# Building the shifted convolution input inside SBUF, with a reordered output projection and column-tiled modulation, in an eight-core encoder block

## The chip, the cores and the metric

The kernel runs on the 8 cores of one Trainium2 chip; every core executes the same program on its own data. The metric is the device time of one execution, in microseconds (us), on the slowest core. Most executions agree within 0.3%, but some fall into a slower state in which the cores of one die (cores 0 to 3 or 4 to 7) are granted a lower TensorE clock. Only fast runs are compared here; where a median quoted below holds a slow run, the text says so.

## The reference, cut to what matters

Each core handles 16384 positions in 32 tiles of 512, in five sequences of 16, 4, 4, 4 and 4 tiles. All widths below are channels.

```python
mod = silu(c) @ w_ada + b_ada;  shift, scale, gate = split(mod, 3)
h = rmsnorm(x, norm_g) * (1 + scale) + shift            # 1024
p = h @ w_in                                            # 3584
a_in, a_b, a_c, a_z, b_v, b_g, b_z = split(p)           # 512 each
y_a = a_b * dwconv3(a_c * a_in) * silu(a_z)
u   = dwconv31(b_v * sigmoid(b_g)) + conv_b_b           # 31 taps, zero padded
y_b = silu(head_layernorm(u)) * silu(b_z)
out = rmsnorm(x + gate * (concat(y_a, y_b) @ w_out), final_g)
```

Two things matter. The 31-tap convolution of tile i needs 15 positions of the neighbouring tiles, so it can only run once the GLU (`u = b_v * sigmoid(b_g)`) of tile i+1 is complete. And the output row needs its own mean square before it can be stored.

## The kernel before

The traces show the engines run their instructions in program order (VectorE's below are an example). A helper records each operation and adds the semaphore waits, so the order of the Python statements is the order on each engine. TensorE does the input projection (w_in), the convolution, the layer-norm sums and the output projection (w_out).

The convolution multiplies 32 channels x 4 shifted copies (128 rows of contraction) by a 128x32 weight block, 8 times with different offsets. The array V with its four shifted copies is made through a scratch array in DRAM:

```python
def u_store(i):                       # 1 DMA: u of this tile to DRAM
    T.dma("sync", ... out=U_d[:, c:c + NT] ..., in_=u[:], reads=[("u", i % 2)], writes=[("U", i)])

def v_load(i):                        # 4 DMAs: V from DRAM, row group k shifted by k
    for k in range(4):
        T.dma("sync", ... out=V[32*k:32*k+32, :, :],
              in_=U_d[:, c + k:c + k + NT + 28].rearrange("(g c) t -> c g t", c=32))
```

Zero padding between the sequences is written to that scratch once, at the start, by six stores, all of which write the same tracked key, so that each waits for the one before:

```python
for s in range(nseq + 1):
    T.dma("sync", ... out=U_d[:, c0:c0 + PAD]..., in_=zpad[:], writes=["Upad"], semkey="upad")
```

The output projection makes eight half blocks (4 blocks of 128 positions x 2 halves of 512 columns). The transposes of the next tile's normalised input stand between the first four. A block's finish (mean square, power, scale, store) is recorded one block late:

```python
def stage_d(i, nxt):
    fin = []
    for sub in range(4):
        for h in range(2):
            if nxt is not None and sub < 2:
                a_T_group(nxt, (sub*2 + h)*2); a_T_group(nxt, (sub*2 + h)*2 + 1)   # transposes
            bank = PB.next()                                          # one of 6 PSUM banks
            for kc in range(8): matmul(bank, yT[:, kc, ...], w_out_sb[:, kc, ...])
            vector: tmp = bank * gate;  gpsimd: xbuf += tmp
        fin.append(block)
        if len(fin) > 1: d_finish(fin.pop(0))     # the finish of the block before
    while fin: d_finish(fin.pop(0))

def d_finish(...):
    scalar: ssE = sum(xbuf**2);  vector: msE = ssE/D + eps
    gpsimd: rsE = msE ** -0.5;   vector: xbuf = xbuf * rsE * fg;  sync: store
```

The main loop, cut, with `prev = i - 1` and `nxt = i + 1`:

```python
a_load(nxt)                                # x of the next tile
for j in range(4): glu(i, j)               # 64 matmuls, u of tile i
u_store(i); v_load(prev); d_loads(prev)
for j in range(4):
    a1(i, j)                               # 64 matmuls, group A inputs
    if j == 0: a_compute(nxt)              # normalisation: ScalarE squares, GpSimd scaling
# conv_b(0..3) of prev, mixed with matmuls of tile i ("a2", "zb") and layer norm
stage_d(prev, nxt)
```

## Time and profile before

| | before |
|---|---|
| time, median of 3 runs (lowest to highest) | 3340.89 us (3325.13 to 3380.62, the last a slow one, 1.7% above the lowest) |
| profiled run, slowest core | 3350.3 us |
| TensorE busy | 2547.4 us, 76% |
| TensorE waiting for V | 582.7 us |
| first convolution matmul starts | 222.57 us |
| average period of one tile after that | 99.75 us |

The first lines are from the page: busy time by engine (part 1), then two groups of matmuls (part 5) with their busy time, mean ns of one, and the idle time before them with what ended most of it.

```profile
PE 2547.4 (76%) x14704; PEld 1122.2 (33%) x14704; DVE 1096.5 (33%) x1718; ACT 1325.9 (40%) x2180; POOL 740.7 (22%) x773
...
L454 PE MATMUL pb<-hT,w_in_sb 128*128 128x512 bf16 x7168 | 1604.3, 382 | 39.6 <-ACT tp L487 37.5
L541 PE MATMUL pb<-V,WC 128*32 128x512 bf16 x4096 | 296.6, 441 | 582.7 <-DMA V<-u_scratch 582.7
```

TensorE (PE) is by far the busiest engine; the others are at 40% or less. What keeps TensorE from being busy is the wait for V. The view of TensorE's waits lists them: who waited, for whom, then us in total, times, longest us.

```profile
PE pb L541 <- DMA V<-u_scratch: 582.7, 32, 26.7
PE pb L607 <- POOL yT L582: 111.4, 64, 4.9
PE pb L454 <- ACT tp L487: 37.5, 1, 37.5
...
PE ptr L308 <- ACT hT L317: 2.6, 3, 1.1
```

The load of V costs about 18 us in each of 32 tiles; the output projection waits 3.5 us a tile for GpSimd's last yT products; and there is one hole of 37.5 us. The timeline of one tile on TensorE shows the first two. Its columns are start, duration, instruction, count, and in brackets the idle time before it with its releaser.

```profile
1526.00 3.61 PE L541 MATMUL pb<-V,WC 128*32 128x512 bf16 x32 [17.65 <-DMA V<-u_scratch]
...
1533.56 1.91 PE L541 MATMUL pb<-V,WC 128*32 128x512 bf16 x32
...
1563.84 0.38 PE L607 MATMUL pb<-w_out_sb,yT 128*128 128x512 bf16 x1 [2.71 <-POOL yT L582]
```

After the wait the first convolution group takes 3.61 us where the second takes 1.91: the granted clock there is 0.50.

VectorE at the end of the same output projection, whose matmuls end at 1580.1:

```profile
1577.49 1.28 DVE L612 TENSOR_TENSOR tp<-pb,gate_bc 128x512 f32<-128x512 f32 x2
...
1581.66 1.28 DVE L635 SCALAR_TENSOR_TENSOR xb<-xb,rsE,fg_bc 128x1024 f32<-128x1024 f32 x1 [2.83 <-POOL rsE L633]
1582.86 1.28 DVE L612 TENSOR_TENSOR tp<-pb,gate_bc 128x512 f32<-128x512 f32 x2
...
1589.18 1.28 DVE L635 SCALAR_TENSOR_TENSOR xb<-xb,rsE,fg_bc 128x1024 f32<-128x1024 f32 x1 [0.80 <-POOL rsE L633]
```

The scaling of one block (L635) waits for GpSimd's power, and the next block's gate multiplies (L612) stand behind it, but they already follow 5.4 us later (1577.49 to 1582.86), and the last block ends at 1590.46, 10.4 us after the matmuls.

Last, the start. The sync engine's DMA issue queue (SPq), then TensorE:

```profile
60.60 48.45 SPq L362 DMA_DIRECT2D u_scratch<-zpad  x6
...
109.77 3.46 SPq L285 DMA_DIRECT2D xb<-x  x4
```

```profile
125.97 23.38 PE L454 MATMUL pb<-hT,w_in_sb 128*128 128x512 bf16 x96 [37.46 <-ACT tp L487]
```

The six zero-pad stores hold the queue for 48 us, tile 1's x is issued only after them, and TensorE stands still for 37.5 us.

### The profile page before, as it was taken

To read this page: it belongs to the slowest core of one execution; us is meant where nothing else is said; L and a number is where in the kernel's file an instruction comes from. 1 tells how busy PE (TensorE), PEld (TensorE's weight loads), DVE (VectorE), ACT (ScalarE), POOL (GpSimd) and SP (SyncE) were. 2 spreads that over 40 slices of the span, in tenths; PEclk is the share of its full clock that TensorE was granted. 3 is DMA by queue.
4 is the path that set the end of the run, shared out by engine and by line. 5 is a ranking of instruction groups with operands and counts; after the bars stand their busy time and mean duration, and the time that the engine had idled before them with its cause. 6 is when DMAs were issued, how large, how long until landed. Compare 5 with 4: busy or idle time off the path is not lost.

```text
span 3350.3 us, 45102 instructions; the slowest of 8 cores (3297.0 to 3350.3 us)
## 1 busy us (share of the span) xinstructions
PE 2547.4 (76%) x14704; PEld 1122.2 (33%) x14704; DVE 1096.5 (33%) x1718; ACT 1325.9 (40%) x2180; POOL 740.7 (22%) x773
## 2 busy tenths in 40 slices
PE   7567787677796788797877788767788677778783
PEld 2223333233343333343333343333334333333331
DVE  1122333233333333333333343323233333333333
ACT  1123444433443433444442444443344343344333
POOL 3002222122222122222212221212222212222212
PEclk9788998888998898898888899888899888899896
DMA  9744323344322443422344423344432344432323
GB/s 191 145 84 108 91 75 76 84 109 109 100 70 60 96 109 109 105 66 66 96 102 115 109 73 94 71 96 109 109 92 81 63 99 109 109 95 77 65 71 102
DMA packets 159060, 317.22 MB, mean 95 GB/s; under 512 B 14570, under 2 KB 105834, under 8 KB 158836
## 3 DMA queue, kind: packets, MB, share of 16 engines
q1 hardware_dynamic: 149332, 304.90, 36.0%
q0 software_dynamic: 9504, 9.44, 2.1%
q8 instruction: 127, 2.08, 0.3%
q14 instruction: 97, 0.79, 0.1%
HBM read 239.73 MB, written 84.00 MB: 97 GB/s over the span
## 4 chain that ended last, share of the span: by engine, by line
PE 49%; DMA 28%; ACT 11%; issue 5%; SPq 3%; POOL 2%; DVE 2%; ACTq 0%; DVEq 0%; POOLq 0%
PE pb L454 26%; DMA V<-u_scratch 19%; PE pb L607 13%; PE pb L541 7%; DMA u_scratch<-u 6%; SPq L478 3%; ACT L571 2%; ACT tp L573 2%; ACT tp L578 2%; PE ptr L308 2%; DMA u_scratch<-zpad 1%; POOL yT L582 1%; ACT tp L574 1%; ACT L575 1%; PE pb L552 1%
## 5 line engine op out<-in xcount | busy, mean ns | idle before, releaser
L454 PE MATMUL pb<-hT,w_in_sb 128*128 128x512 bf16 x7168 | 1604.3, 382 | 39.6 <-ACT tp L487 37.5
L454 PEld LDWEIGHTS pb<-hT,w_in_sb 128*128 128x128 bf16 x7168 | 702.6, 98 | 905.9 <-issue 95.5
L541 PE MATMUL pb<-V,WC 128*32 128x512 bf16 x4096 | 296.6, 441 | 582.7 <-DMA V<-u_scratch 582.7
L607 PE MATMUL pb<-w_out_sb,yT 128*128 128x512 bf16 x2048 | 516.7, 404 | 111.4 <-POOL yT L582 111.4
L582 POOL TENSOR_TENSOR yT<-tp,gb 128x512 bf16<-128x512 f32 x128 | 145.0, 1154 | 1604.0 <-ACT tp L578 1604.0
L546 ACT ACTIVATE sq<-pb,cbb_sb 128x512 bf16<-128x512 f32 x128 | 87.3, 682 | 904.9 <-PE pb L541 904.9
L614 POOL TENSOR_TENSOR xb<-tp,xb 128x512 f32<-128x512 f32 x256 | 323.9, 1265 | 340.4 <-DVE tp L612 304.8
L508 DVE TENSOR_TENSOR ga<-pb,tp 128x512 bf16<-128x512 f32 x128 | 88.5, 692 | 894.1 <-PE pb L454 783.6
L541 PEld LDWEIGHTS pb<-V,WC 128*32 128x32 bf16 x4096 | 113.6, 107 | 747.8 <-issue 685.0
L607 PEld LDWEIGHTS pb<-w_out_sb,yT 128*128 128x128 bf16 x2048 | 206.8, 104 | 368.1 <-issue 182.2
L629 ACT ACTIVATE tp<-xb 128x1024 bf16<-128x1024 f32 x128 | 135.0, 1055 | 366.9 <-POOL xb L614 366.9
L612 DVE TENSOR_TENSOR tp<-pb,gate_bc 128x512 f32<-128x512 f32 x256 | 170.5, 686 | 278.1 <-PE pb L607 243.8
L635 DVE SCALAR_TENSOR_TENSOR xb<-xb,rsE,fg_bc 128x1024 f32<-128x1024 f32 x128 | 164.4, 1284 | 272.7 <-POOL rsE L633 272.7
L529 DVE SCALAR_TENSOR_TENSOR tp<-t,caT_sb,tp 128x512 f32<-128x512 bf16 x256 | 193.0, 754 | 28.4 <-DVE tp L526 0.9
L292 ACT ACTIVATE xs<-xb 128x1024 bf16<-128x1024 f32 x128 | 135.1, 1056 | 92.3 <-DMA xb<-x 87.3
L317 ACT ACTIVATE hT<-ptr,shT,gsT 128x512 bf16<-128x512 bf16 x124 | 96.2, 776 | 164.2 <-PE ptr L308 164.2
L489 DVE TENSOR_TENSOR t<-pb,tp 128x512 bf16<-128x512 f32 x128 | 88.9, 694 | 208.5 <-PE pb L454 157.6
L297 POOL TENSOR_TENSOR rsA<-msA,mhalf 128x4 f32<-128x4 f32 x32 | 32.5, 1017 | 537.7 <-DVE msA L295 537.7
L577 DVE TENSOR_TENSOR tp<-tp 128x512 f32<-128x512 f32 x128 | 85.5, 688 | 199.1 <-ACT tp L574 199.1
L487 ACT ACTIVATE tp<-pb 128x512 f32<-128x512 f32 x128 | 74.0, 591 | 185.1 <-PE pb L454 179.2
L300 POOL TENSOR_SCALAR xs<-xb,rsA 128x1024 bf16<-128x1024 f32 x128 | 140.9, 1119 | 7.4 <-POOL rsA L297 6.7
L463 ACT ACTIVATE tp<-pb 128x512 f32<-128x512 f32 x128 | 72.5, 590 | 135.1 <-PE pb L454 134.8
(70 smaller groups left out, 1609.1 us busy)
## 6 DMA issues: line engine op xcount, KB each, us to landing
xb<-x SPq DMA_DIRECT2D x256, 512.0 KB, 9.0
V<-u_scratch SPq DMA_DIRECT2D x128, 540.0 KB, 15.2
y<-xb SPq DMA_DIRECT2D x128, 512.0 KB, 2.9
u_scratch<-u SPq DMA_DIRECT2D x32, 512.0 KB, 8.2
xb<-w_ada SPq DMA_DIRECT2D x24, 512.0 KB, 5.2
w_in_sb<-w_in POOLq DMA_DIRECT2D x14, 512.0 KB, 25.5
gate_bc<-gate_scratch SPq DMA_DIRECT2D x5, 512.0 KB, 5.1
w_out_sb<-w_out POOLq DMA_DIRECT2D x4, 512.0 KB, 51.0
```

Source lines behind the costliest of these rows:

```text
L292: T.op("scalar", lambda e, xbuf=xbuf, sub=sub: e.activation(out=xs[:, sub, :], in_=xbuf[:], func=AF.Square, accum_out=ssA[:, sub:sub + 1]) ...
L300: T.op("gpsimd", lambda e, xbuf=xbuf, sub=sub: e.tensor_scalar(out=xs[:, sub, :], in0=xbuf[:], scalar1=rsA[:, sub:sub + 1], scalar2=1.0, o ...
L454: T.op("tensor", lambda e, bank=bank, kc=kc: e.matmul(bank[:], lhsT=w_in_sb[:, kc, col0:col0 + 128], rhs=hT[:, kc, :], start=(kc == 0), st ...
L478: T.dma("sync", lambda e, k=k: e.dma_start(out=V[32 * k:32 * k + 32, :, :], in_=U_d[:, c + k:c + k + NT + 28].rearrange("(g c) t -> c g t" ...
L529: T.op("vector", lambda e, k=k: e.scalar_tensor_tensor(out=acc[:], in0=t1[:, j, k:k + NT], scalar=caT[:, j * KA + k:j * KA + k + 1], in1=a ...
L541: T.op("tensor", lambda e, p=p, g=g: e.matmul(bank[32 * g:32 * g + 32, :], lhsT=WC[:, (j * 4 + g) * 8 + p, :], rhs=V[:, j * 4 + g, 4 * p:4 ...
L582: T.op("gpsimd", lambda e, cc=cc, gsrc=gsrc, j=j: e.tensor_tensor(out=yT[:, 4 + j, :], in0=cc[:], in1=gsrc, op=ALU.mult), reads=[ckey, gke ...
L607: T.op("tensor", lambda e, bank=bank, kc=kc, sub=sub, h=h: e.matmul(bank[:], lhsT=yT[:, kc, sub * 128:(sub + 1) * 128], rhs=w_out_sb[:, kc ...
L612: T.op("vector", lambda e, tmp=tmp, bank=bank, h=h: e.tensor_tensor(out=tmp[:], in0=bank[:], in1=gate_bc[:, h * NT:(h + 1) * NT], op=ALU.m ...
L614: T.op("gpsimd", lambda e, tmp=tmp, xbuf=xbuf, h=h: e.tensor_tensor(out=xbuf[:, h * NT:(h + 1) * NT], in0=tmp[:], in1=xbuf[:, h * NT:(h + ...
L629: T.op("scalar", lambda e: e.activation(out=jb[:].bitcast(BF16), in_=xbuf[:], func=AF.Square, accum_out=ssE[:, c:c + 1]), reads=[xkey], wr ...
L635: T.op("vector", lambda e: e.scalar_tensor_tensor(out=xbuf[:], in0=xbuf[:], scalar=rsE[:, c:c + 1], in1=fg_bc[:], op0=ALU.mult, op1=ALU.mult),
```

## The change

Its intent is to take DRAM out of the way from u to V. u gets room for its neighbours' 15 positions (544 columns). Twelve DMAs copy u, shifted, from SBUF to SBUF, in runs of about 4 KB per partition, and four unshifted blocks are copied by VectorE. With this the zero-pad stores go. The output projection first does contraction halves 0 to 3 (y_a, ready early) of the first four half blocks, with transposes between, and then all the rest, so as not to wait for the last yT. The modulation uses four 32-column tiles of the array at once.

The V path:

```diff
-def u_store(i): ... U_d <- u          # 1 DMA
-def v_load(i):  ... V <- U_d          # 4 DMAs, 1 KB rows
+def u_halo(i):                        # 15 columns to and from the neighbour tile
+    T.op("gpsimd", tensor_copy(out=up[:, :, NT+15:NT+30], in_=u[:, :, 15:30]))
+    T.op("gpsimd", tensor_copy(out=u[:, :, 0:15], in_=up[:, :, NT:NT+15]))
+def v_fill(i):
+    for k in range(4):
+        for g in range(4):
+            sh = 2 * ((k - g) % 4)
+            if k == g: T.op("vector", tensor_copy(V[32*g:32*g+32, g], u[32*g:32*g+32]))
+            else:      T.dma("sync", V[32*k:32*k+32, g] flat [0:4*UW-sh] <- u[32*g:32*g+32] flat [sh:4*UW])
```

The output projection:

```diff
-            if nxt is not None and sub < 2: two transposes groups
-            for kc in range(8): matmul
-            evacuate (gate multiply, add)
-        fin.append(block)
-        if len(fin) > 1: d_finish(*fin.pop(0))
+for n in range(4):
+    if nxt is not None:
+        a_T_group(nxt, 2*n); a_T_group(nxt, 2*n + 1)
+    d_mm(n, range(4))
+for n in range(8):
+    d_mm(n, range(4, 8) if n < 4 else range(8))
+    d_evac(n)                # gate multiply, add, and for h == 1 at once: d_finish(...)
```

The last line hides a side effect: the finish of a block is no longer one block late. The main loop and the start:

```diff
-a_load(nxt)
 for j in range(4):
     glu(i, j)
-u_store(i); v_load(prev); d_loads(prev)
+    if j == 1: a_compute(nxt)
+u_halo(i); v_fill(prev); a_load(i + 2); d_loads(prev)
 ...
     a1(i, j)
-    if j == 0: a_compute(nxt)
-zero-pad stores to U_d
+memset of both u buffers
+a_load(1)                # at the start, ahead of the weight loads
-mod_piece: matmul(bank[0:nseq, :], lhsT=scT[:, kc, :] (5 columns), rhs, ...)          # fp32
+matmul(mbank[32*q:32*q+32, :], lhsT=scT[:, kc, :] (32 columns), rhs, tile_position=(0, 32*q))
```

(The weight table of the convolution is reordered to match the new shifts; the bias and the transposes of the modulation follow the new layout.)

## The prediction

> **What bounds it now.** TensorE, with holes. Page part 1: TensorE 2547 of 3350 us, ScalarE 40%, VectorE 33%. Waits view: 582.7 us before the 31-tap convolution, 32 times, released by the load of V from the DRAM scratch; 111.4 us in the output projection, released by GpSimd's last yT products. One tile in the timeline (1526-1620 us; period about 100): convolution section 33, projection 21, GLU and A inputs 29, wait for V 18. In the wait, u goes to DRAM (8-9 us), then V comes back in 1 KB rows, queued with x loads (13-23 us). Afterwards the first convolution group takes 3.61 instead of 1.91 us, the next 16 matmuls 4.0 instead of 3.6: 2 us of cold clock, granted 0.50 (windows view). That agrees with the Trainium skill, "TensorE: Matmul & The Clock Gate", Part 1: an idle array restarts at half rate.
>
> **The V path.** u is complete 15 us after the GLU matmuls start; V is wanted at 29. Twelve copies of 139 KB: 0.45 us each to issue (small loads in the trace), so 5.4, then 3 to land (y stores: 2.9). The skill's "SBUF — State Buffer", Door 1, gives 32 partitions 8 of 16 ports, about 218 GB/s: 3.8 to 7.6 us of transfer in all, an estimate no run shows yet. Together 8-10 us where 31 were. The four VectorE copies: 0.6 us each.
>
> **Where part is lost.** (1) The halo copies stand on GpSimd behind the next tile's normalisation (5.4 us), whose ScalarE squares (5 us) now stand between the second and third tanh. (2) A row block's finish now follows its own evacuation at once. VectorE works in order, so the next block's gate multiply waits for multiply 0.7, two GpSimd adds 2.7, square 1.25, mean 0.15, power 0.55, scale 1.3 plus semaphores: 7.3 us per block instead of 5.4. The four end 19 us after the projection's matmuls instead of 10.5. PSUM banks come free late, TensorE stalls about 7 us inside the GLU, u is complete only near 25. Halo copies end at 30, V lands at 38; the convolution starts 38-40 us after the projection instead of 47.
>
> **Projection order.** Worth almost nothing. Before the second of four transpose pairs TensorE needs a transpose bank that ScalarE empties only after the second norm pair and the z gates (timeline: 1563.96-1564.74), the same moment as the last yT (1564.8). I expect the 111 us to become waits of transposes on ScalarE, 3.5-4 us a tile.
>
> **Start.** Six zero-pad stores hold the DMA issue queue 48 us; tile 1's x waits behind them, then ScalarE, then TensorE (37.5 us). That goes. Column tiling takes 32 fp32 gate matmuls (12 us) nearly out of tile 1; the first modulation is bound by its weight loads: 1-2 us. First convolution at 160 instead of 222 us. The tail gains nothing.
>
> **Sum.** 30 periods save about 8.5 us each (18 wait + 2 cold - 7 bank stalls - 2 to 3 remaining wait - 1.5 new cold clock): 250. Start 60. Tail +4. 3341 - 306 = about 3030 us; 8 in 10 between 2880 and 3140. Faster by over 2%: 0.96; within 2%: 0.03; slower: 0.01.
>
> **What will show it.** Wait for V below 120 us in total; GLU matmuls waiting for evacuations 4-8 us a tile; VectorE waiting for GpSimd's power above 4 us per block; transposes waiting for ScalarE near 110 us; no 37.5 us hole.
>
> **What would make it wrong.** SBUF copies that serialise on few ports (+8 us a tile, 3270); slow VectorE copies; a block chain that overlaps better than I think (near 2800); a clock throttled once TensorE is denser (dense stretches now get 1.00).

## The result, and the profile after

| | before | after |
|---|---|---|
| time, median | 3335.17 us (4 runs, one of them slow at 3380.62) | 3130.31 us (4 runs, 3127.92 to 3134.56) |
| ratio of fast runs | 1 | 0.9397 (95%: 0.9365 to 0.9428) |
| profiled run, slowest core | 3350.3 us | 3129.9 us |
| TensorE busy | 2547.4 us | 2618.9 us |
| first convolution | 222.57 us | 168.72 us |
| average period of one tile | 99.75 us | 94.15 us |

A ratio is the mean time of one kernel's fast runs over that of the other's fast runs in the same rounds, so it is not quite the ratio of the medians quoted. The outputs were correct, as in all runs below. The time lies inside the predicted range, 10 us from its upper end and 100 us above the predicted 3030.

The difference of the profiled spans, 220.4 us, divides so: start 53.9 (222.57 − 168.72), 30 periods of 5.60 each (168), the last interval 4.2, and 5.6 lost after the last tile's convolution starts (55.3 to 60.9).

The page of after, same lines:

```profile
PE 2618.9 (84%) x14724; PEld 1137.7 (36%) x14724; DVE 1209.6 (39%) x1848; ACT 1325.1 (42%) x2178; POOL 784.9 (25%) x838
...
L444 PE MATMUL pb<-hT,w_in_sb 128*128 128x512 bf16 x7168 | 1665.6, 390 | 200.3 <-DVE tp L617 158.3
...
L542 PE MATMUL pb<-V,WC 128*32 128x512 bf16 x4096 | 313.9, 423 | 102.8 <-DMA V<-u 100.9
```

The same 7168 input-projection matmuls are busy for 61 us longer (1665.6 against 1604.3) and the same convolution matmuls for 17. TensorE did no more of this work; most of the extra time is a lower clock. The clock records say how much: at 0.50 TensorE was busy for 340 us (before 272), which costs half of that time, and at 0.81 for 140 us (before none), which costs 3/16 of it. That makes 196 us against 136, so 60 of the 72 us by which TensorE's busy time grew. (The mean granted clock of the span, 0.919 against 0.883, hides this: before stood at 0.50 for 788 us, but 516 of them were waits.) That is why its busy share, 84%, overstates the gain. The Trainium skill, "Trainium Kernel Development and Optimization", Best Practices, says to judge the distance to the peak by MFU (the share of peak arithmetic) and weight-load busy share, not by matmul busy share; PEld rose only from 33% to 36%.

TensorE's waits in after:

```profile
PE pb L444 <- DVE tp L617: 158.3, 58, 3.5
PE ptr L303 <- ACT hT L312: 126.3, 33, 4.5
PE pb L542 <- DMA V<-u: 100.9, 40, 28.8
...
PE pb L607 <- POOL yT L583: 3.7, 4, 1.6
```

The wait for V fell from 582.7 to 100.9 us; without the first (6.6) and last (28.8) it is 65.5 over 30 tiles, 2.2 us a tile. The projection's 111.4 us on yT fell to 3.7, but 126.3 us of transposes waiting for ScalarE stand in their place. And 158.3 us are new: GLU matmuls waiting for a PSUM bank until VectorE's gate multiply (L617) has emptied it. The timeline of TensorE from the end of a projection (224.97) to the convolution:

```profile
224.97 3.62 PE L444 MATMUL pb<-hT,w_in_sb 128*128 128x512 bf16 x16
231.04 3.61 PE L444 MATMUL pb<-hT,w_in_sb 128*128 128x512 bf16 x16 [2.45 <-DVE tp L617]
238.15 22.82 PE L444 MATMUL pb<-hT,w_in_sb 128*128 128x512 bf16 x96 [3.50 <-DVE tp L617]
263.15 4.24 PE L542 MATMUL pb<-V,WC 128*32 128x512 bf16 x32 [2.19 <-DMA V<-u]
```

VectorE in the same stretch:

```profile
230.21 1.28 DVE L617 TENSOR_TENSOR tp<-pb,gate_bc 128x512 f32<-128x512 f32 x2
235.17 0.15 DVE L642 TENSOR_SCALAR msE<-ssE 128x1 f32<-128x1 f32 x1 [3.68 <-ACT tp L640]
236.12 1.28 DVE L646 SCALAR_TENSOR_TENSOR xb<-xb,rsE,fg_bc 128x1024 f32<-128x1024 f32 x1 [0.80 <-POOL rsE L644]
237.32 1.28 DVE L617 TENSOR_TENSOR tp<-pb,gate_bc 128x512 f32<-128x512 f32 x2
...
254.26 2.97 DVE L476 COPY V<-u 32x2176 bf16<-32x2176 bf16 x4 [4.14 <-POOL u L464]
```

Between two pairs of gate multiplies VectorE now waits for the whole chain of the block's finish: from 230.21 to 237.32 is 7.11 us where before had 5.4, and the last block ends at 244.52, 19.6 us after the projection's matmuls where before had 10.4. The multiply at 237.32 is the one that TensorE waits for until 238.15; its own matmuls had ended by 224.97, so it stood behind the scaling at 236.12 and not behind TensorE.

GpSimd and the DMA issue queue then show how V is made:

```profile
249.57 4.40 POOL L295 TENSOR_SCALAR xs<-xb,rsA 128x1024 bf16<-128x1024 f32 x4 [0.23 <-POOL rsA L292]
253.92 0.23 POOL L464 COPY u<-u 128x60 bf16<-128x60 bf16 x1
```

```profile
254.33 7.66 SPq L479 DMA_DIRECT2D V<-u  x12
```

u is complete at 250.1, but the halo copy stands on GpSimd behind the next tile's normalisation until 253.92. Twelve copies then take 7.66 us to issue, and each lands 2.6 to 2.7 us after its issue (median).

The second pair of transposes of a projection in after, and the matmuls behind it:

```profile
302.21 1.01 PE L303 MATMUL ptr<-ident,xs 128*128 128x128 bf16 x8 [4.19 <-ACT hT L312]
303.01 1.91 PE L607 MATMUL pb<-w_out_sb,yT 128*128 128x512 bf16 x4
```

Only four early matmuls (297.00 to 298.03) run before this pair stops TensorE for 4.19 us, and the four matmuls behind it take 1.91 us where those took 1.03. The start, tile 0 on TensorE:

```profile
73.54 48.54 PE L444 MATMUL pb<-hT,w_in_sb 128*128 128x512 bf16 x212 [2.17 <-DMA w_in_sb<-w_in]
```

The hole of 37.5 us is gone: 212 of the 224 input-projection matmuls of tile 0 run without a break. Last, the windows view: the length of the stretch, busy time of PE, PEld, DVE, ACT and POOL, then the granted clock, the DMA share and GB/s.

```profile
261.00:263.10 2.10, 0.00 (x0) 0.00 (x0) 1.18 (x2) 0.00 (x0) 0.40 (x2) 1.00 0.88 201
...
263.20:265.20 2.00, 1.97 (x11) 0.67 (x15) 1.78 (x3) 0.00 (x0) 0.00 (x0) 0.50 0.96 328
302.20:307.20 5.00, 4.99 (x24) 2.89 (x25) 1.09 (x2) 1.56 (x2) 0.00 (x0) 0.50 0.00 0
```

During the 2.2 us wait for V the clock is still 1.00; just as the convolution starts it falls to 0.50. The projection, after its 4.19 us wait, also runs at 0.50.

### The profile page after: what moved, and what is told of

Its sections match the earlier page's. It is cut to its first block, busy times and chain, and to the rows that moved or that the text cites. A ratio compares the mean times of both kernels' runs of the same rounds, so it can differ in the third digit from the quotient of the medians.

```text
span 3129.9 us, 46443 instructions; the slowest of 8 cores (3106.7 to 3129.9 us)
## 1 busy us (share of the span) xinstructions
PE 2618.9 (84%) x14724; PEld 1137.7 (36%) x14724; DVE 1209.6 (39%) x1848; ACT 1325.1 (42%) x2178; POOL 784.9 (25%) x838
## 4 chain that ended last, share of the span: by engine, by line
PE 35%; ACT 19%; POOL 15%; issue 14%; DVE 6%; SPq 5%; DMA 5%; DVEq 1%; ACTq 0%; POOLq 0%
PE pb L444 19%; POOL xb L619 10%; PE pb L542 8%; SPq L479 5%; PE pb L607 5%; ACT tp L640 4%; DVE tp L617 3%; DMA V<-u 3%; POOL xs L295 3%; ACT L572 2%; PE ptr L303 2%; ACT tp L574 2%; ACT tp L579 2%; POOL rsE L644 2%; ACT tp L575 1%
## 5 line engine op out<-in xcount | busy, mean ns | idle before, releaser
L444 PE MATMUL pb<-hT,w_in_sb 128*128 128x512 bf16 x7168 | 1665.6, 390 | 200.3 <-DVE tp L617 158.3
L542 PE MATMUL pb<-V,WC 128*32 128x512 bf16 x4096 | 313.9, 423 | 102.8 <-DMA V<-u 100.9
L303 PE MATMUL ptr<-ident,xs 128*128 128x128 bf16 x1024 | 104.9, 263 | 128.1 <-ACT hT L312 126.3
L488 ACT ACTIVATE tp<-pb 128x512 f32<-128x512 f32 x128 | 76.4, 597 | 296.3 <-PE pb L444 291.8
L642 DVE TENSOR_SCALAR msE<-ssE 128x1 f32<-128x1 f32 x128 | 19.7, 154 | 462.0 <-ACT tp L640 462.0
L617 DVE TENSOR_TENSOR tp<-pb,gate_bc 128x512 f32<-128x512 f32 x256 | 167.3, 684 | 53.7 <-PE pb L607 50.1
L316 DVE TENSOR_SCALAR hT<-ptr,gsT,shT 128x512 bf16<-128x512 bf16 x124 | 67.3, 542 | 247.4 <-PE ptr L303 247.4
L303 PEld LDWEIGHTS ptr<-ident,xs 128*128 128x128 bf16 x1024 | 89.4, 122 | 182.2 <-issue 174.9
L295 POOL TENSOR_SCALAR xs<-xb,rsA 128x1024 bf16<-128x1024 f32 x128 | 148.3, 1177 | 7.4 <-POOL rsA L292 7.0
```

Of the source, the lines that this page charges most:

```text
L295: T.op("gpsimd", lambda e, xbuf=xbuf, sub=sub: e.tensor_scalar(out=xs[:, sub, :], in0=xbuf[:], scalar1=rsA[:, sub:sub + 1], scalar2=1.0, o ...
L303: T.op("tensor", lambda e, sub=sub: e.transpose(out=pt[:, sub * 128:(sub + 1) * 128], in_=xs[:, sub, kc * 128:(kc + 1) * 128], identity=id ...
L444: T.op("tensor", lambda e, bank=bank, kc=kc: e.matmul(bank[:], lhsT=w_in_sb[:, kc, col0:col0 + 128], rhs=hT[:, kc, :], start=(kc == 0), st ...
L542: T.op("tensor", lambda e, p=p, g=g: e.matmul(bank[32 * g:32 * g + 32, :], lhsT=WC[:, (j * 4 + g) * 8 + p, :], rhs=V[:, g, j, TAP0[p]:TAP0 ...
L617: T.op("vector", lambda e: e.tensor_tensor(out=tmp[:], in0=bank[:], in1=gate_bc[:, h * NT:(h + 1) * NT], op=ALU.mult), reads=[bkey, "gate_ ...
```

## The experiments

The theory after reading this trace: after's V path works, and the 100 us are lost to the block finish at once (bank stalls), to the halo copy behind the normalisation, and to cold clocks that follow the short waits. Rivals: the loss comes from the new order of the projection itself; from copies in SBUF that are slow in themselves; from the modulation.

Medians of the stages of a tile, worked out from each kernel's timeline of TensorE ("GLU, A" runs from the projection's end to the first convolution matmul; "first group" from there to the next other matmul; the period is an average):

| kernel | conv section | projection | GLU, A to conv | first group | period | time, us |
|---|---|---|---|---|---|---|
| before | 33.25 | 20.95 | 45.63 | 3.54 | 99.75 | 3335 |
| after | 33.84 | 22.48 | 38.18 | 4.40 | 94.15 | 3130 |
| late_finish | 33.74 | 22.52 | 30.35 | 4.52 | 85.97 | 2874 |
| old_projection | 32.43 | 21.03 | 28.50 | 3.20 | 82.19 | 2768 |
| halo_early | 31.07 | 21.60 | 36.05 | 1.85 | 88.96 | 2979 |
| v_path_only | 33.87 | 20.69 | 30.37 | 4.63 | 85.01 | 2853 |
| old_projection_halo_early | 31.07 | 21.38 | 27.72 | 1.85 | 80.30 | 2711 |
| halves_before_transposes | 31.08 | 16.98 | 27.72 | 1.85 | 76.0 | 2576 |
| short_runs | 33.96 | 22.45 | 38.33 | 4.55 | 94.26 | 3139 |

### 1. late_finish: after, with the finish one block later

```diff
                 if h == 1:
-                    d_finish(xbuf, xkey, i * NT + sub * 128)
+                    fin.append((xbuf, xkey, i * NT + sub * 128))
+                    if len(fin) > 1: d_finish(*fin.pop(0))
```

> The kernel after, with one thing changed: a row block's finish is issued one block later, as before the change had it. My theory (the VectorE chain of the finish holds PSUM banks): finish chain about 5.5 us per block instead of 7.3, TensorE's waits inside the GLU for VectorE (158 us in the kernel after) fall under 30 us, the period falls from 94 to 87 us or so: 2900 to 2960 us. Rival (the GLU stalls come from the ScalarE squares moved between the tanh's): bank waits stay, time within 1% of 3130 us.

One of five executions was fast, 2874.19 us (the slow ones: 2908.25 to 3089.3), so there is no interval; the profile is of the fast one. TensorE's waits no longer have an entry for VectorE's gate multiply; in the GLU 11.4 us are left, on VectorE's u. The two largest entries are:

```profile
PE ptr L303 <- ACT hT L312: 129.1, 34, 4.5
PE pb L542 <- DMA V<-u: 97.9, 48, 21.3
```

The period fell by 8.2 us, all of it between projection and convolution. The finish at once costs after about 250 us (30 × 8.2), more than the 158 us of waits that the profile shows under that name. The clock records hold most of the rest: half rate costs 3.5 us a period instead of 5.2, and no core here shows the stretch at 0.81 that cost after 0.9. On core 0, which has none in after either, the period fell by 8.1 us, so the 8.2 do not rest on that stretch. The result is faster than I expected.

### 2. old_projection: after, with the whole output projection of before

```diff
-        def stage_d(...)   # that of after
+        def stage_d(...)   # that of before
```

> The kernel after, with the projection stage of before (eight matmuls per bank in a row, transposes between them, late finish). Against late_finish this differs only in the order of the half products. My theory: the half order is worth nothing, because a transpose waits for ScalarE at the same moment; so within 1% of late_finish, the waits move back from transposes to the last yT products. Rival: the half order saves its 111 us, then this is 80 to 110 us slower than late_finish.

Two fast runs, 2768.48 and 2775.88 us (two slow: 2881.23, 3022.04); ratio to before 0.8317 (0.8268 to 0.8367). The waits:

```profile
PE pb L608 <- POOL yT L583: 111.8, 64, 5.3
PE pb L542 <- DMA V<-u: 61.7, 54, 21.7
```

I had expected the order alone to matter less than 1%. It matters 3.8 us a tile against late_finish (85.97 to 82.19): after's half-by-half order is worse than that of before, even with the finish late. The traces show one way: in late_finish the first gate multiply comes 12.5 us after the stage's start (1073.64 to 1086.09), in old_projection 6.3 us (1036.49 to 1042.77), so that the finish chain ends 11.8 instead of 10.4 us after the last matmul, u is complete later, and V is waited for longer (97.9 against 61.7 us in all). The new order only exchanges a wait of 112 us for yT for one of 129 us in front of the transposes.

### 3. halo_early: after, with the normalisation behind the halo copies

```diff
-                    if j == 1 and nxt is not None:
-                        a_compute(nxt)
                 u_halo(i)
             if prev is not None:
                 v_fill(prev)
+            if cur_ok and nxt is not None:
+                a_compute(nxt)
```

> The kernel after, with the next tile's normalisation issued after the halo copies and V copies instead of inside the GLU. My theory: the halo copies then follow the last u directly, V is there before TensorE wants it; the 101 us wait for V and about 2 us a tile of cold clock behind it go, the bank stalls in the GLU stay: 3000 to 3050 us. Rival (V is limited by the copies' issue and landing, not by when u is complete): 3110 to 3130 us.

2979.28 us (2976.65 to 2983.34), ratio 0.894 (0.8907 to 0.8972), a little faster than expected. V is waited for only at the start and the end (35.5 us in 4 waits); the bank stalls stay (178.4 us). The period fell by 5.2 us: 2.1 between projection and convolution, 2.8 in the convolution section, and 0.9 in the projection (medians; their sum is not quite the average). The first convolution group now takes 1.85 us instead of 4.40. Of the 5.2 us, 0.9 is the stretch at 0.81 in after's trace, which no core of halo_early shows. On core 0, which has none in either run, the period fell by 4.5 us (93.39 to 88.88): the wait for V was 2.0 us, the cost of half rate fell by 3.1 (5.2 to 2.1), and the GLU's waits grew by 0.9. So a wait of 2 us cost about 5. That is the term that the prediction had too small. (The edit also takes the squares out of the GLU; what that alone does was not tested.)

### 4. v_path_only: before, with the V path of after and nothing else

> The kernel before with the V path alone: the SBUF copies, halo copies and taps, no zero-pad stores; normalisation, projection, finish and modulation as before. My theory: u is complete 15 us after the projection, V lands near 25 us and is wanted at 29, so the wait and its cold clock go (20 us a tile) with no bank stalls, and the 37 us hole at the start goes: 2650 to 2780 us, clearly faster than the whole change (3130). Rival (the other parts of the change are needed for the gain): 3100 us or more.

(The edit takes `u_halo`, `v_fill`, the new convolution weights and the removal of the zero-pad stores from after, and leaves projection, normalisation, x loads and modulation as before.) Two fast runs, 2852.66 and 2854.81 us (two slow: 2870.19, 3070.58), ratio 0.8562 (0.8513 to 0.861): 280 us faster than the whole change, but slower than the 2650 to 2780 that I expected. The DMA issue queue shows why:

```profile
1091.84 2.11 SPq L279 DMA_DIRECT2D xb<-x  x4
1096.25 7.34 SPq L478 DMA_DIRECT2D V<-u  x12
```

The convolution starts at 1111.65 after a wait of 3.00 us for V, 8 us after the last copy was issued. By the page of this run the copies land 8.3 to 8.4 us after their issue (median), where those of after need 2.6 to 2.7. With before's placement four x loads (0.5 MB each) are issued just ahead of the copies; after issues them behind. This is a part of the change that helps. (Experiment 5 confirms it, though it differs from this run in the modulation and a little in the place of the normalisation too.)

### 5. old_projection_halo_early: experiments 2 and 3 together

> Two parts of the change undone together: the projection stage of before (old_projection) and the normalisation after the halo copies (halo_early). old_projection alone has a period of 82.2 us with 62 us of waits for V and cold convolution groups. If the two losses are separate, V is now always in time: period 79 to 80 us, fast runs 2680 to 2720 us. Against v_path_only (85.0 us) this differs mainly in the x loads issued behind the V copies; if v_path_only was slow because its V copies queued behind x loads, this one shows no wait for V. Rival (V late for another reason, such as its own issue): wait for V stays above 60 us, 2760 us or more.

2711.16 us (three fast runs, 2709.68 to 2711.19; one slow, 2736.78), ratio 0.8106 (0.8052 to 0.816), inside the expectation. V is waited for twice only (28.5 us, start and end), and the first group takes 1.85 us. With x loads issued behind the copies the V path costs TensorE nothing in the middle of the run. What is left is the wait of 109.4 us for yT in the projection, followed by eight matmuls that take 3.62 us where the next eight take 1.89.

### 6. halves_before_transposes: all four first halves, then the transposes; late finish; halo early

```diff
             for n in range(4):
-                if nxt is not None:
-                    a_T_group(nxt, 2 * n)
-                    a_T_group(nxt, 2 * n + 1)
                 d_mm(n, range(4))
             for n in range(8):
+                if nxt is not None and n < 4:
+                    a_T_group(nxt, 2 * n)
+                    a_T_group(nxt, 2 * n + 1)
                 d_mm(n, range(4, 8) if n < 4 else range(8))
```

> As old_projection_halo_early, but the four first halves of the projection run ahead of all transposes, and each transpose pair goes with a second half; finish one block later. My theory (the half order was worthless because a transpose stood between the halves): 3.5 us of matmuls now fill the stall of 3.4 us, so 1.5 to 2.5 us a tile faster than old_projection_halo_early (50 to 80 us). Rival (halves only delay the first gate multiply and the finish chain): equal or slower.

2575.65 us (2574.63 to 2576.08), ratio 0.7702 (0.7659 to 0.7744): the fastest of all, faster than both kernels. TensorE is busy 94% of the span and PEld 42%. The timeline of one projection:

```profile
1039.10 3.62 PE L608 MATMUL pb<-w_out_sb,yT 128*128 128x512 bf16 x16
1042.56 0.61 PE L303 MATMUL ptr<-ident,xs 128*128 128x128 bf16 x8
1043.09 1.01 PE L608 MATMUL pb<-w_out_sb,yT 128*128 128x512 bf16 x3
1044.84 0.38 PE L608 MATMUL pb<-w_out_sb,yT 128*128 128x512 bf16 x1 [0.74 <-POOL yT L583]
```

Sixteen matmuls (3.6 us) now stand where TensorE used to wait; one wait of 0.74 us is left and the clock stays up. The stage shrinks from 21.4 to 17.0 us: 2.7 of the 4.4 are waits (109.4 − 26.9 us, over 31 tiles), the rest is clock: half rate costs 0.1 us a period instead of 2.3. The period fell by 4.3 us. So the intent of the projection's reorder was sound; interleaving the transposes with the early halves spoilt it. I had expected 1.5 to 2.5 us a tile.

### 7. halves_finish_at_once: experiment 6 with the finish at once

```diff
-                    if len(fin) > 1:
-                        d_finish(*fin.pop(0))
+                    d_finish(*fin.pop(0))
```

> halves_before_transposes with one thing put back: a block's finish issued at once after its own evacuation, as the change has it. My theory: the chain is again 7.3 us per block, the four end about 18 us after the projection's last matmul, TensorE waits for VectorE inside the GLU come back at 5 to 8 us a tile: 2740 to 2830 us. Rival (the late finish only helped because the projection's halves were slow): within 2% of 2576 us.

Three fast runs, 2846.47 to 2847.43 us (three slow), ratio 0.8506 (0.8444 to 0.8567); 271 us slower than experiment 6, and 17 above the range that I expected. The profile fell in the slow state of die 0 (its cores 3077 us at clock 0.839); core 6, on the other die (median of its cores 2842 us, 0.951), waited so in the two largest entries:

```profile
PE ptr L303 <- ACT hT L312: 96.9, 33, 3.4
PE ptr L303 <- DVE hT L316: 54.9, 31, 2.0
```

The finish at once costs as much here as in after, but I had expected the stall at the GLU's banks again, and it sits at the transposes, with only 25 us left in the GLU: their evacuations on ScalarE and VectorE stand in line behind the square and the scaling of block 0. The stage that grew is the projection, 24.35 us against 16.98 (medians). The cost follows from the in-order queue; where it surfaces depends on what stands behind.

### 8. short_runs: after, with the copies in four runs of about 1 KB

```diff
-   V[32*k:32*k+32, g] flat [0:4*UW-sh]  <- u[32*g:32*g+32] flat [sh:4*UW]
+   V[32*k:32*k+32, g, :, 0:UW-6]        <- u[32*g:32*g+32, :, sh:UW-6+sh]
```

> The kernel after with the twelve V copies in four runs of about 1 KB per partition instead of one of 4.3 KB; bytes the same. If the run length makes the copies quick: 1 KB rows cost about 0.1 us each per engine in the kernel before (2048 rows in 13 us), so V lands about 5 us later, landing above 5 us, time 3230 to 3290 us. If what mattered was only to leave out the trip through DRAM: landing 2.7 to 3.5 us and time within 1% of 3130 us.

3139.2 us (three fast runs, 3133.16 to 3143.02; one slow, 3183.85), ratio 0.9373 (0.9293 to 0.9453), period 94.26 against 94.15. The copies land 2.5 us after issue (median) instead of 2.6 to 2.7 and take 8.1 us to issue instead of 7.5; from the first issue to the last landing it is 10.3 against 10.2 us. The length of the runs, 4.3 or 1 KB, plays no part here; shorter ones were not tried. This agrees with the Trainium skill, "DMA: Bandwidth & Descriptors", section "Why small descriptors are slow (HBM only)", which says that transfers between SBUF and SBUF don't suffer the penalty of small pieces.

### 9. old_modulation: after, with the modulation of before

> The kernel after with the modulation of before (no column tiles). Prediction on record: the gate matmuls cost about 10 us in tile 1 and 1 to 2 us in the first modulation: 3138 to 3145 us, first convolution at about 180 us instead of 169. Rival (v_path_only kept the old modulation and reached its first convolution at 173 us): 3 to 5 us, 3133 us. Either way inside 1%.

(The edit restores the 5-row fp32 matmuls for shift, scale and gate, with their bias and transposes.) 3134.34 us (three fast runs, 3120.09 to 3141.36; one slow, 3169.11), ratio 0.9359 (0.9291 to 0.9427). The first convolution comes at 176.38 us instead of 168.72, between what the prediction (about 11 us later) and the rival (3 to 5) had; the average period is 93.69 against 94.15. Column tiling is worth some 8 us at the start, which the run-to-run spread of the total hides.

### 10. pads_other_queue: before, with the zero-pad stores on GpSimd's queue

> The kernel before with one thing changed: the six zero-pad stores are issued from GpSimd's queue behind the weight loads instead of the queue that also issues tile 1's x loads. My theory: the 37.5 us hole of tile 0 goes, first convolution near 185 us instead of 222, 3295 to 3305 us. Rival (the x loads come late because the weights fill the DMA engines): hole mostly stays, 3325 us or more.

3348.0 us (three fast runs, 3340.03 to 3353.46; one slow, 3400.1), ratio 0.9998 (0.9894 to 1.0103). Tile 1's x loads are issued at 45.70 us instead of 109.77, yet nothing is gained. The experiment was confounded: GpSimd now waits for the stores itself, one after the other; its timeline, second and third store:

```profile
128.78 0.76 POOL L362 DMA_DIRECT2D u_scratch<-zpad  x1 [65.36 <-DMA u_scratch<-zpad]
131.47 0.75 POOL L362 DMA_DIRECT2D u_scratch<-zpad  x1 [1.94 <-DMA u_scratch<-zpad]
```

Its normalisation of tile 1 comes at 145.35, and TensorE's hole has only moved. It shows, all the same, that it is the wait of each store for the one before, above all for the first, that holds a queue.

### 11. pads_after_x: before, with the zero-pad stores on the same queue behind tile 1's x loads

> The kernel before with the zero-pad stores left on the same issue queue but placed behind tile 1's x loads (pads_other_queue moved the hole to GpSimd, since each pad store waits for the one before it, so it tested nothing cleanly). My theory: x arrives in time, nothing waits for the pads before V of tile 0, first convolution near 190 us instead of 222, about 1% less time: 3295 to 3315 us. Rival (the start is bound by the weight loads): first convolution above 210 us, within 0.5% of before.

3314.05 us (five fast runs, 3305.43 to 3336.2; one slow, 3398.65), ratio 0.993 (0.9897 to 0.9962). The 37.5 us hole is gone (the x loads issue at 45.76; 212 matmuls run from 70.03 without a break), but the first convolution comes only 21.5 us earlier, at 201.05, after a wait of 24.68 us for V: part of what the hole cost is paid again at the next wait.

## Why the prediction was right or wrong

The direction and most of the mechanisms held; the size was 100 us short.

**What held.** The wait for V was predicted below 120 us in total and is 100.9; u complete near 25 us after the projection (25.1); the convolution 38 to 40 us after it (38.2). The finish at once was costed at 7.3 us a block (7.1), ending 19 us after the matmuls (19.6), with 7 us of bank stalls a tile (158.3 and the smaller GLU waits, 14.2 and 9.5, are 182 us or about 6 a tile). The 111 us of the projection moved to transposes (126.3). The hole of 37.5 us went.

**The term that was mis-sized: the clock.** The sum "18 wait + 2 cold − 7 bank stalls − 2 to 3 remaining wait − 1.5 new cold clock", given as 8.5 us a period, measured 5.60. Its waits came out as predicted: over the thirty periods of the profiled cores TensorE's idle time fell by 8.7 us a period (the wait for V by 15.5, against 6.1 of new waits in the GLU and 0.7 in the projection and layer norm). But TensorE's busy time rose by 3.1 us a period for the same work, where the prediction had 2 − 1.5 = 0.5 saved. By the clock records half rate cost it 5.2 us a period (4.0 in before) and the stretch at 0.81 another 0.9; 1.1 us are not assigned. The prediction took the cold restart as something that shrinks with the wait. In fact the 2 us were not saved: a wait of 2.2 us left the first convolution group at 4.40 us where before's 18 us left it at 3.54, and the convolution section at 33.84 (before 33.25). The other waits, 2.5 and 3.5 us in the GLU and 4.2 us in the projection, brought cold stretches of their own in places. Experiment 3 shows it from the other side: with the wait for V gone, half rate costs 2.3 us a period instead of 5.2. The thirty periods were forecast to save 250 us and saved 168, which is 82 us of the miss. The remaining difference is mostly (15 us) that before's profiled run (3352 us as timed) is itself slower than its median of 3335.

A smaller part is the stretch at 0.81. It stands in the records of cores 2 to 5, two cores of each die, 150 us on each; cores 0, 1, 6 and 7 have none, and their periods are 93.3 to 93.6 us against 94.15. On the profiled core 1505 to 1525 us shows 0.81 with TensorE busy throughout, and one period there takes 98.8 us (1488.81 to 1587.59). The prediction named a throttled clock as a risk. The value agrees with the peak-current limiter at 13/16 in the Trainium skill, "TensorE: Matmul & The Clock Gate", Part 1; but denser is not more throttled here, as the densest kernel (experiment 6) was granted 1.00 for 500 us on end.

**The step that failed: "Projection order. Worth almost nothing."** That the wait would move from yT to the transposes was right. That this made the order neutral was wrong in both directions. With transposes between the halves it costs 3.8 us a tile (experiment 2 against 1), and with the halves ahead of all transposes it gains 4.3 (experiment 6 against 5). Had I asked which matmuls need nothing from the stalled engines, and how many of them there were (16, 3.6 us, against a stall of 3.5), the better order was there to be seen.

**The start.** Predicted 160 us, measured 168.7. Of the 53.9 us gained, 21.5 belong to the pads (experiment 11), about 18 to the shorter wait for V (24.7 to 6.4 us) and some 8 to the modulation (experiment 9); about 6 are not assigned. After waits 18.0 us for w_in where before waited 0.7, in a stretch that before spent on other waits; whether the 9 us lie there was not tested. The tail: +4 predicted, 5.6 measured.

**Where the gain went that the change could have had.** The V path alone gives 2853; with x loads behind the copies and the halo copies ahead of the normalisation the same path gives 2711. The change put 420 us of that back on, by the finish at once (about 250 us), the order of the halves (about 115, 30 × 3.8), and the normalisation ahead of the halo copies (57 after old_projection, about 150 in after itself, where it coincides with the late u). These overlap and do not add up.

**Which waits bring the clock down.** The 2.2 us before the convolution is followed by 0.50, while one of 2.45 us in the GLU was followed by 16 matmuls at full speed (3.61 us) and one of 3.50 us by a mean of 0.67. The clock records settle this. On after's profiled core every stretch at 0.50 starts on one fixed grid with steps of 3.41 us and lasts a whole number of steps. Four steps around these waits (the third column is TensorE's busy time, the clock is the third number from the end):

```profile
229.08:232.49 3.41, 1.45 (x7) 0.71 (x8) 2.41 (x3) 0.00 (x0) 1.27 (x1) 1.00 0.37 151
235.91:239.32 3.41, 1.17 (x6) 0.61 (x7) 2.48 (x3) 0.00 (x0) 1.22 (x2) 1.00 0.31 127
239.32:242.73 3.41, 3.41 (x10) 1.18 (x9) 0.15 (x1) 1.70 (x4) 1.57 (x3) 0.50 0.07 26
259.80:263.21 3.41, 1.22 (x7) 0.40 (x5) 1.19 (x3) 0.19 (x1) 0.40 (x2) 1.00 0.89 205
```

The wait of 2.45 us (228.59 to 231.04) is cut by an edge of the grid and leaves 1.96 us idle in its step: the clock stays. The wait of 3.50 us leaves 2.24 us in one step, and the 2.2 us before the convolution lie in one step whole (2.19): the next step runs at 0.50. On this core, from 100 us on, the 83 steps before a fall of the clock had 1.73 us idle or more (75 of them 2.0 or more), and the 640 steps after which it stayed at 1.00 had 2.04 us at most. On all cores of before, after and experiments 1 to 6, 94% of 2857 falls follow 2.0 us or more, and 63 of 43861 steps without a fall exceed 2.0. So about 2 us of idle time within one step decides (to some tenths of a us; the ends of matmuls in the trace are modelled), and whether a wait costs clock depends on where it falls on the grid.

**Open.** Why some kernels fell into the slow state more often (four of five executions of experiment 1, none of experiment 6), and why after had stretches at 0.81. The two may be one thing: in the one profile taken in the slow state (experiment 7) the four cores of die 0 stand at 0.81 for 1815 to 1914 us and those of die 1 never do.

## What to carry to other kernels

On in-order engines, finish a block one block later: work that waits for a chain of other engines must not stand ahead of the evacuation that frees a PSUM bank or a transpose buffer, and independent matmuls belong ahead of everything that needs the engine that is late. Count a wait of TensorE with the restart after it: here a wait of 2 us cost about 5. And try the parts of a bundled change alone: here one part by itself (2853 us) beat the bundle (3130), and the parts put in a better order gave 2576.

## What the Trainium skill lacked or had wrong

- "TensorE: Matmul & The Clock Gate", Part 1, gives the cold state after at least one idle window of about 3.4 us, free-running. The clock records here show a fixed grid of 3.41 us, but a step of it need not be idle throughout: about 2 us are enough (83 falls on after's profiled core after 1.73 us or more, none after 640 steps with 2.04 us at most). TensorE waited for V in 27 of 32 tiles, about 2 us or more each, and in all 27 a stretch at 0.50 overlaps the first convolution group (median 4.40 us against 1.85 without the wait). The section gives no cost for such partly idle windows.
- The same section says that the ramp penalty is under 1% of a typical kernel span, of a kernel's warm-up. That figure does not carry over to restarts in every tile: here TensorE was busy at 0.50 for 340 us of after's 3130, which costs it 170 us or 5.4%.
- The same section says to budget a clock of 13/16 for sustained dense matmuls on all cores. Here the densest kernel (experiment 6) had TensorE busy 489 of 500 us from 1000 to 1500 at a granted clock of 1.00, and a mean of 0.981 to 0.985 on all eight cores over the whole span.
- "SBUF — State Buffer", Door 1, has 32 partitions reach half the ports. The estimate from it, 3.8 to 7.6 us of transfer for twelve copies, was not what bound them: they took 7.5 us (median) to issue from one queue and each landed 2.6 to 2.7 us later, the last one no later than the others (2.8). No page that I used says how long one issue holds the queue, which decided here: about 0.6 us.
- No page that I used has a figure for what a small copy pays behind large loads: behind four x loads of 0.5 MB the V copies landed 8.3 to 8.4 us after their issue instead of 2.6 to 2.7 (experiment 4).
